# A two-layer decoder trunk: one plain feed-forward block fewer, and two unit heads side by side

## The chip, the cores and the metric

The kernel runs on one core of a Trainium2 chip. The metric is the device time of one launch in microseconds; before the change it is 1261.36 us, the median of three runs (1261.36 to 1261.72). TensorE multiplies, VectorE (DVE), ScalarE (ACT) and GpSimd (POOL) do the elementwise work, SyncE (SP) issues nearly all loads. Each engine takes its instructions in the order in which the program lists them.

## The reference

What is computed: two layers of a hybrid decoder on 512 tokens with 16 learned meta tokens ahead, model width 1024, float32.

```python
def hybrid_layer(h, ...):
    proj = rmsnorm(h, attn_norm_g) @ w_in          # 8 heads of forgetting attention, 4 of retention
    mix = concatenate([fox_out, silu(rg) * groupnorm(ret)], -1)
    h = h + mix @ w_out
    hn = rmsnorm(h, ffn_norm_g)
    ff = silu(hn @ w_gate) * (hn @ w_up)           # d_ff = 2816 = 22 blocks of 128
    return h + ff @ w_down
```

In the second layer only the 512 real tokens are needed after the attention's keys and values, and a final RMSNorm follows.

## The kernel before

**Layout.** Channels lie on the 128 partitions, tokens along the free dimension: `h` is 8 tiles of 128 x 528. Each float32 factor of a product is split into a rounded part `hi` and a rest `lo`, both of a type that TensorE takes at full rate, and a product is three matmuls: hi x hi, hi x lo, lo x hi. So each weight tile of 128 x 1024 that is loaded (`raw`) is cast by ScalarE (`whi`) and subtracted by VectorE or GpSimd (`wlo`) before TensorE can use it. A job is one such weight tile. Layer 0 takes all 528 columns as two matmuls of 264, layer 1 the 512 real ones as one matmul of 512.

**The feed-forward (`ffn`, lines 842 to 1264).** The 22 blocks of 128 hidden channels are computed in one of two ways.

- A *plain* block (`f < PLAIN`, three of them) is two jobs of `dense_steps`, gate and up, over the 8 input tiles: 96 matmuls of 264 columns in layer 0, 48 of 512 in layer 1. `g_done` scales the gate's sums and applies silu, `u_done` multiplies and splits the result into the activations `ah`, `al`.
- A *unit* (class `Unit`, line 937) does gate and up together by a Strassen-like scheme with seven half products instead of eight, 84 matmuls of half the columns (264 in layer 0, 256 in layer 1). Its four weight forms `w1` to `w4` are jobs of their own: `w1` is the gate weights, `w2` and `w3` are sums and differences of gate and up weights that VectorE makes in `make2` and `make3` (`S`, `fraw`), `w4` comes from `make4`. Its parts on TensorE are `head` (24 matmuls with `w1`, plain tokens `xh`, `xl`), `middle` (36, with `w2` and half of `w3`) and `tail` (24, with the rest of `w3` and `w4`). `middle` and `tail` need the token forms `th`, `tl`, which `x_forms` makes for four pairs of input tiles on ScalarE and VectorE while the plain blocks run. A unit holds one bank of `psa` (four banks in all) and one two-bank accumulator of `psd` (two in all); `done` (line 1002) reads it with the addition of line 1006.

**Down products.** Blocks are gathered in rounds (`ROUNDS`). When a round is complete, each of the 8 tiles of `h` gets the round's part of the down projection: four jobs of two tiles each. They are put into the next round: a unit's middle, the first down product, the unit's tail, the second down product (lines 1079 to 1106). `tails` and the loop at line 1102 serve the units that have no such job and the jobs that are left over. In layer 1 the last round is done in two column parts (272 and 240) together with the final norm.

**What sets the order.** TensorE's instructions stand in the order in which the steps are written. The other engines' are placed by a list scheduler: of what is ready by its own clock it takes what comes first in the program; `high_priority` moves a piece ahead. Buffers come from rings: `raw` has three, `whi`/`wlo` and the units' second ring `fwhi`/`fwlo` two each, jobs alternating between the two rings. `dense_steps` (line 205) casts the next job's weights at steps 1 and 4 of a job (`convert(j + 1)`), `need` (line 912) those of a unit's job and up to two after it. Steps put in from line 1259 on place the token forms and the RMS statistics among the first steps.

Of the kernel before, what the change touches and what calls it, by code (L numbers as in the profile page):

```python
# [11 lines left out]
F32R = mybir.dt.float32r  # L12
# [27 lines left out]
def hybrid_kernel(ctx, tc, x_t, w_in, w_fl, w_out, w_gate, w_up, w_down, vecs, b_fg, rope, decay, mask, ident, out_t):  # L40
# [127 lines left out]

    def wring(tag):
        pool = phase["ffn"] if tag[0] == "f" else wp  # L170
        return pool.tile([128, NK, 128], F32R, name=tag, tag=tag, bufs=2)

    def convert(j, upto=NK, pinned=False):

        if j >= len(jobs):
            return
        job = jobs[j]
        fetch(j)
        if "make" in job:
# [12 lines left out]
        while job["split"] < min(n, upto):  # L192
            c0 = job["split"]
            c1 = min(n, c0 + (2 if j < 2 and c0 < 4 else 4))
            size, hi, lo = job["w"][c0 // job["w"][0][0]]
            o = c0 % size
            hi, lo = hi[:, o:o + c1 - c0], lo[:, o:o + c1 - c0]
            with tc.high_priority() if j == 5 else ExitStack():
                pin(nc.scalar.copy(hi, job["raw"][:, c0:c1]), pinned)  # L199
            step = 1 if job["pool"] else c1 - c0  # L200
            for c in range(0, c1 - c0, step):
                pin(sub(lo[:, c:c + step], job["raw"][:, c0 + c:c0 + c + step], hi[:, c:c + step].bitcast(F32)), pinned)  # L202
            job["split"] = c1

    def dense_steps(src, parts, pool=False, banks=False, ahead=(1, 4), own=None, wait=None):

# [5 lines left out]
        def chunk(k0, k, n, xs, cols, ps, done):  # L212
            def go():
# [621 lines left out]
    def out_proj(l, rnd, mix, real):  # L835

        cols = REAL if real else FULL
        xs = lambda k: mix[k]["mix"]
        return sum([dense_steps(w_out[l, rnd, m2], [(4 * s, xs, 4, cols, add_h(2 * m2 + s, real)) for s in range(2)],
                                rnd == 0 or m2 < 2, rnd == 1 and m2 == 1) for m2 in range(NK // 2)], [])  # L840

    def ffn(l, st, real, last):
        QC = REAL if real else FULL
# [93 lines left out]
        class Unit:  # L937
# [23 lines left out]
            def make2(self, hi, lo):  # L961
                a, b = self.t["a"], self.t["b"]
                s = self.t["s"] = fft("S", F32, (128, NK, 128), 2)
                nc.vector.tensor_add(s[:, HB:NK], b[:, 0:HB], b[:, HB:NK])
                nc.vector.tensor_sub(s[:, 0:HB], s[:, HB:NK], a[:, 0:HB])
                splits(hi, lo, s)


            def make3(self, hi, lo):
# [104 lines left out]
            return [chunk(k) for k in range(n)]  # L1074

        steps = []
        tails = []
        fills = []
        for r, (f0, f1) in enumerate(ROUNDS):
            for f in range(f0, f1):  # L1080
                if f < PLAIN:
                    steps += dense_steps(w_gate[l, f], [(0, xs, NK, QC, g_done(f) if f else held.append)], banks=f == 1)
                    steps += dense_steps(w_up[l, f], [(0, xs, NK, QC, u_done(f))])
                    continue
                u = Unit(f)
                steps += u.head()
                for v in tails:
                    v.last()
                    steps += v.tail()
                tails = []  # L1090
                u.rest()
                steps += u.middle()
                if fills:
                    p, g0, g1 = fills.pop(0)
                    j = down_job(p, g0, g1)
                    steps += down(j, 0, 2 * p, g0, g1, not real)
                    u.last()
                    steps += u.tail()
                    steps += down(j, 1, 2 * p + 1, g0, g1, False)
                else:  # L1100
                    tails = [u]
            for p, g0, g1 in fills:
                j = down_job(p, g0, g1)
                for s in range(2):
                    steps += down(j, s, 2 * p + s, g0, g1, False)
            fills = [(p, f0, f1) for p in range(NK // 2)]
        n = f1 - f0
        js = [down_job(p, f0, f1) for p, _, _ in fills]
# [349 lines left out]
```

## Time and profile before

| | |
|---|---|
| median of three runs | 1261.36 us |
| profiled execution | 1261.38 us |
| its span, first to last instruction | 1259.6 us |
| mean granted clock of TensorE | 0.998 |
| idle time of TensorE | 10.9 us, of it 2.1 in the first 50 us and 8.5 in the last 60 |
| bytes moved | 116.19 MB, 92 GB/s |

The span is 1.8 us shorter than the time of the execution. The profile has one row for each group of instructions with its engine, line and tiles; PE is TensorE, PEld its weight loads, which run beside the matmuls, DVE VectorE. An instruction is shown by its start and its length, and since instructions overlap a little on their engine, the spacing of starts says how fast a queue moves. The chain of waits follows the work that ended last back to its beginning. A table of waits says who waited for whom.

### The profile page before, as it was taken

What the parts mean: (1) busy time and instruction counts of PE and PEld (TensorE: products, weight loads), DVE (VectorE), ACT (ScalarE), POOL (GpSimd) and SP (SyncE); (2) the same over time, 40 slices, a digit from 0 to 9 for tenths busy, and PEclk for the clock granted to TensorE, in tenths of its full rate; (3) what the DMA queues carried; (4) which work ended last, traced back from release to release, by engine and by line L of the source; (5) the groups of instructions that cost most, each with busy time, mean ns of one, the idle gap of its engine ahead of it and who ended that gap; (6) DMA issues with size and microseconds to landing.
All of it is one profiled execution on the core that took longest, in us unless ns stands there. A gap on an engine that the chain in (4) does not pass through costs nothing.

```text
span 1259.6 us, 23534 instructions
## 1 busy us (share of the span) xinstructions
PE 1248.7 (99%) x9225; PEld 1191.9 (95%) x9225; DVE 989.2 (79%) x1786; ACT 706.6 (56%) x1307; POOL 281.6 (22%) x552
## 2 busy tenths in 40 slices
PE   9999999999999999999999999999999999999997
PEld 8999999999999999999999988998789999999996
DVE  7887756789888888887786876567899888888867
ACT  7767655776454444444466665557764444444445
POOL 4545655420000000000125556554100000000000
PEclk9999999999999999999999999999999999999999
DMA  6222222123233323332322222221333333333322
GB/s 219 68 76 71 74 68 90 55 81 117 93 102 103 96 100 101 101 101 85 103 75 84 76 77 70 82 77 51 130 95 111 101 101 101 100 101 101 101 84 67
DMA packets 43342, 116.19 MB, mean 92 GB/s; under 512 B 5088, under 2 KB 12000, under 8 KB 43232
## 3 DMA queue, kind: packets, MB, share of 16 engines
q1 hardware_dynamic: 42800, 114.41, 28.4%
q8 instruction: 72, 1.18, 0.4%
q14 instruction: 38, 0.31, 0.1%
q10 hardware_dynamic: 432, 0.29, 0.1%
HBM read 112.58 MB, written 2.10 MB: 91 GB/s over the span
## 4 chain that ended last, share of the span: by engine, by line
PE 95%; DVE 3%; ACT 2%; DMA 0%; issue 0%; ACTq 0%; DVEq 0%
PE psd L225 31%; PE psa L930 18%; PE psd L1065 14%; PE psd L930 13%; PE psa L225 5%; PE psa L1065 4%; PE psa L441 2%; PE psa L608 2%; PE psa L538 1%; PE psa L742 1%; PE psa L778 1%; PE psa L402 1%; PE psa L304 0%; DMA raw<-w_in 0%; PE psa L617 0%
## 5 line engine op out<-in xcount | busy, mean ns | idle before, releaser
L202 POOL TENSOR_TENSOR wlo<-raw,whi 128x128 fp32r<-128x128 f32 x504 | 262.4, 555 | 243.0 <-ACT whi L199 220.9
L225 PE MATMUL psd<-xh,whi 128*128 128x264 f32 (+1 forms) x792 | 195.2, 314 | 0.1
L225 PE MATMUL psd<-xh,wlo 128*128 128x264 f32 (+1 forms) x792 | 186.6, 303 | 0.0
L225 PE MATMUL psd<-xl,whi 128*128 128x264 f32 (+1 forms) x792 | 186.2, 302 | 0.2 <-DVE xl L341 0.2
L225 PEld LDWEIGHTS psd<-xh,wlo 128*128 128x128 f32 x792 | 126.8, 188 | 6.3 <-DVE wlo L202 0.4
L225 PEld LDWEIGHTS psd<-xh,whi 128*128 128x128 f32 x792 | 128.1, 189 | 4.9 <-ACT whi L199 0.6
L225 PEld LDWEIGHTS psd<-xl,whi 128*128 128x128 f32 x792 | 127.3, 188 | 4.8 <-DVE xl L341 0.9
L199 ACT CAST whi<-raw 128x512 fp32r<-128x512 f32 (+1 forms) x168 | 98.2, 613 | 42.9 <-PE psd L225 29.2
L918 ACT CAST whi<-raw 128x1024 fp32r<-128x1024 f32 (+2 forms) x62 | 54.9, 885 | 51.3 <-PE psd L930 39.8
L918 ACT CAST fwhi<-raw 128x1024 fp32r<-128x1024 f32 (+2 forms) x62 | 55.6, 897 | 47.5 <-PE psd L930 40.0
L122 POOL MEMSET kc<- 64x528 f32 x4 | 2.1, 533 | 345.6 <-PE psa L930 345.4
L919 DVE TENSOR_TENSOR wlo<-raw,whi 128x1024 fp32r<-128x1024 f32 (+2 forms) x62 | 62.9, 1015 | 12.3 <-ACT whi L918 12.2
L919 DVE TENSOR_TENSOR fwlo<-raw,fwhi 128x1024 fp32r<-128x1024 f32 (+2 forms) x62 | 64.0, 1032 | 10.1 <-ACT fwhi L918 10.0
L930 PE MATMUL psa<-th,whi 128*128 128x264 f32 (+1 forms) x232 | 65.4, 282 | 0.0
L930 PE MATMUL psa<-th,wlo 128*128 128x264 f32 (+1 forms) x232 | 65.4, 282 | 0.0
L930 PE MATMUL psa<-tl,whi 128*128 128x264 f32 (+1 forms) x232 | 65.3, 282 | 0.0
L930 PE MATMUL psa<-th,fwhi 128*128 128x264 f32 (+1 forms) x224 | 63.4, 283 | 0.0
L930 PE MATMUL psa<-tl,fwhi 128*128 128x264 f32 (+1 forms) x224 | 63.3, 283 | 0.0
L930 PE MATMUL psa<-th,fwlo 128*128 128x264 f32 (+1 forms) x224 | 63.2, 282 | 0.0
L555 ACT ACTIVATE pr<-pr,nmax 128x144 f32<-128x144 f32 (+1 forms) x64 | 36.8, 576 | 45.5 <-DVE nmax L542 26.0
L918 ACT CAST fwhi<-S 128x1024 fp32r<-128x1024 f32 x20 | 21.0, 1049 | 68.6 <-PE psa L930 66.5
L996 ACT COPY e<-psa 128x264 f32<-128x264 f32 (+1 forms) x114 | 42.8, 375 | 28.3 <-PE psa L930 24.1
(366 smaller groups left out, 4041.1 us busy)
## 6 DMA issues: line engine op xcount, KB each, us to landing
raw<-w_in SPq DMA_DIRECT2D x54, 512.0 KB, 3.5
raw<-w_gate SPq DMA_DIRECT2D x44, 512.0 KB, 3.9
fraw<-w_up SPq DMA_DIRECT2D x38, 512.0 KB, 3.5
raw<-w_down SPq DMA_DIRECT2D x64, 256.0 KB, 2.9
raw<-w_out SPq DMA_DIRECT2D x16, 512.0 KB, 3.5
raw<-w_down SPq DMA_DIRECT2D x32, 192.0 KB, 2.5
raw<-w_up SPq DMA_DIRECT2D x6, 512.0 KB, 3.5
h<-x_t SPq DMA_DIRECT2D x8, 264.0 KB, 4.9
```

The costliest lines, as they stand in the source:

```text
L199: pin(nc.scalar.copy(hi, job["raw"][:, c0:c1]), pinned)
L202: pin(sub(lo[:, c:c + step], job["raw"][:, c0 + c:c0 + c + step], hi[:, c:c + step].bitcast(F32)), pinned)
L225: nc.tensor.matmul(ps[1][b][:, 0:c1 - c0], w[:, wk, :], x[:, c0:c1], start=(k == 0 and i == 0), stop=(k == n - 1 and i == 2))
L402: nc.tensor.matmul(ps[:, 0:c1 - c0], wf[k // HB][:, k % HB, :], st["x"][k][part][:, c0:c1], start=(i == 0), stop=(i == 2 * NK - 1))
L441: nc.tensor.transpose(ps[:, 128 * j:128 * j + 128], src[:, o:o + 128], idt)
L555: nc.scalar.activation(pr, pr, AF.Exp, bias=nmax[0:nq], scale=-1.0, accum_out=rsum)
L608: nc.tensor.matmul(po[:, c0:SEQ], v[:, j, :], pp[:, j, META + c0:T], start=(j == 0 and i == 0), stop=(j == 4))
L918: nc.scalar.copy(hi, src)
L919: nc.vector.tensor_sub(lo, src, hi.bitcast(F32))
L930: nc.tensor.matmul(bank()[:, 0:b.shape[-1]], a[:, o + k, :], b, start=(fresh and k == 0 and i == 0), stop=(k == n - 1 and i == 2), skip_gr ...
L996: nc.scalar.copy(self.t["e"][:, i], self.t["x"][:, 0:w])
L1065: nc.tensor.matmul(v[:, 0:c1 - c0], a[:, s * n + k, :], b[:, c0:c1], start=(k == 0 and i == 0), stop=(k == n - 1 and i == 2))
```

## The change

In both layers the feed-forward has two plain blocks instead of three, so the units begin with block 2. The rounds are 2 blocks and five times 4 instead of 3, four times 4 and 3: each round's four down jobs now fall on four units, and `tails` and the loop for left-over jobs are gone. At the first unit the heads of blocks 2 and 3 are both issued before the first `middle`, so two units are open at once; for these two units the first down product goes to two `psa` banks in layer 1 as well. `make2` of block 2 is put at high priority. The rings `whi` and `wlo` get three buffers. Dense jobs of the feed-forward's start cast two jobs ahead (`far`), GpSimd instead of VectorE subtracts for one more job of the second output projection (`m2 < 3`), and the token forms stand 7 steps apart instead of 9.

```diff
-ROUNDS = ((0, 3), (3, 7), (7, 11), (11, 15), (15, 19), (19, 22))
-PLAIN = 3
+ROUNDS = ((0, 2), (2, 6), (6, 10), (10, 14), (14, 18), (18, 22))
+PLAIN = 2
...
-        return pool.tile([128, NK, 128], F32R, name=tag, tag=tag, bufs=2)
+        return pool.tile([128, NK, 128], F32R, name=tag, tag=tag, bufs=2 if tag[0] == "f" else 3)
...
-                [(NK, *[wp.tile([128, NK, 128], F32R, name=i, tag=i) for i in ("whi", "wlo")])]
+                [(NK, *[wring(i) for i in ("whi", "wlo")])]
...
                 for half, at_step in enumerate(ahead):
                     if k0 + k == at_step:
                         convert(j + 1, 4 * half + 4)
+                        if far:
+                            convert(j + 2, 4 * half + 4)
...
-                                rnd == 0 or m2 < 2, rnd == 1 and m2 == 1) for m2 in range(NK // 2)], [])
+                                rnd == 0 or m2 < 3, rnd == 1 and m2 == 1, far=rnd == 1 and m2 > 1) for m2 in range(NK // 2)], [])
...
             def make2(self, hi, lo):
...
+                with tc.high_priority() if self.f == PLAIN else ExitStack():
+                    nc.vector.tensor_add(s[:, HB:NK], b[:, 0:HB], b[:, HB:NK])
+                    nc.vector.tensor_sub(s[:, 0:HB], s[:, HB:NK], a[:, 0:HB])
+                    splits(hi, lo, s)
...
-                    steps += dense_steps(w_gate[l, f], [(0, xs, NK, QC, g_done(f) if f else held.append)], banks=f == 1)
-                    steps += dense_steps(w_up[l, f], [(0, xs, NK, QC, u_done(f))])
+                    steps += dense_steps(w_gate[l, f], [(0, xs, NK, QC, g_done(f) if f else held.append)], banks=f == 1, far=True)
+                    steps += dense_steps(w_up[l, f], [(0, xs, NK, QC, u_done(f))], far=f == 0)
                     continue
-                u = Unit(f)
-                steps += u.head()
-                for v in tails:
-                    v.last()
-                    steps += v.tail()
-                tails = []
+                for i in (f, f + 1) if f == PLAIN else (f,):
+                    if i not in units:
+                        units[i] = Unit(i)
+                        steps += units[i].head()
+                u = units[f]
                 u.rest()
                 steps += u.middle()
...
+                p, g0, g1 = fills.pop(0)
                 j = down_job(p, g0, g1)
+                steps += down(j, 0, 2 * p, g0, g1, not real or f < PLAIN + 2)
+                u.last()
+                steps += u.tail()
+                steps += down(j, 1, 2 * p + 1, g0, g1, False)
...
-            steps.insert(NK + 4 + 9 * i, x_forms(i))
+            steps.insert(NK + 4 + 7 * i, x_forms(i))
```

**VectorE ahead of block 3's head, layer 0.** In before, `wlo_4558` is the low part of block 3's gate weights (`w1`), `wlo_4488` that of the third plain block's up weights, `fwlo_4605` block 3's `w2`. The queue around it is:

```order
L202 TENSOR_TENSOR wlo_4488<-raw_4485,whi_4487 128x512
L874 TENSOR_TENSOR tq_4465<-tq_4465,sg_4396 128x528
L895 SCALAR_TENSOR_TENSOR S_4503<-h7_80,vec_84,S_4503 128x264
L202 TENSOR_TENSOR wlo_4488<-raw_4485,whi_4487 128x512
L151 TENSOR_TENSOR al1_4469<-tq_4465,ah1_4468 128x528
L964 TENSOR_TENSOR S_4606<-fraw_4555 128x512
L151 TENSOR_TENSOR tl1_4288<-S_4503,th1_4287 128x1056
L865 SCALAR_TENSOR_TENSOR sg_4537<-psd_4472,R_4273 128x528
L919 TENSOR_TENSOR wlo_4558<-raw_4553,whi_4557 128x1024
```

In the changed kernel `wlo_4495` is block 2's `w2`, made from `S_4496`, and `fwlo_4491` the low part of block 3's gate weights:

```order
L967 TENSOR_TENSOR S_4496<-fraw_4360 128x512
L897 SCALAR_TENSOR_TENSOR S_4459<-h7_80,vec_84,S_4459 128x264
L968 TENSOR_TENSOR S_4496<-S_4496,raw_4358 128x512
L875 SCALAR_TENSOR_TENSOR tq_4479<-psd_4422,R_4287 128x528
L151 TENSOR_TENSOR tl1_4302<-S_4459,th1_4301 128x1056
L921 TENSOR_TENSOR wlo_4495<-S_4496,whi_4494 128x1024
L876 TENSOR_TENSOR tq_4479<-tq_4479,sg_4410 128x528
L921 TENSOR_TENSOR fwlo_4491<-raw_4486,fwhi_4490 128x1024
L151 TENSOR_TENSOR al1_4483<-tq_4479,ah1_4482 128x528
```

The low part for block 3's head now stands behind all four token forms, as before, and behind the whole of block 2's `make2` and `w2`; the dense halves between have gone, and `al1` stands behind it.

**TensorE at the first unit's second down product, layer 0.** In before the first unit (block 3) ends its tail in `psd_4631`, and the second down product goes to `psd_4768`, the other accumulator:

```order
L930 MATMUL psd_4631<-xh7_4148,whi_4676 128x264
L930 MATMUL psd_4631<-xl7_4149,whi_4676 128x264
L930 MATMUL psd_4631<-xh7_4148,wlo_4677 128x264
L1065 MATMUL psd_4768<-ah0_4326,fwhi_4647 128x264 x2
L1065 MATMUL psd_4768<-al0_4327,fwhi_4647 128x264 x2
```

In the changed kernel block 2 ends its tail in `psd_4516`, block 3's head has filled the other accumulator (`psd_4549`), and `psd_4677` lies in the banks of `psd_4516`:

```order
L932 MATMUL psd_4516<-xh7_4162,fwhi_4594 128x264
L932 MATMUL psd_4516<-xl7_4163,fwhi_4594 128x264
L932 MATMUL psd_4516<-xh7_4162,fwlo_4595 128x264
L1068 MATMUL psd_4677<-ah0_4340,whi_4565 128x264 x2
L1068 MATMUL psd_4677<-al0_4341,whi_4565 128x264 x2
```

The rows read alike, but the first matmul of `psd_4677` can start only when the addition that reads `psd_4516` has run. That addition stands in VectorE's queue behind these (`fwlo_4649` is block 3's `w3`, `S_4780` belongs to block 4):

```order
L1073 TENSOR_TENSOR h0_73<-psa_4621,h0_73 128x264
L967 TENSOR_TENSOR S_4780<-fraw_4744 128x512
L968 TENSOR_TENSOR S_4780<-S_4780,raw_4742 128x512
L974 TENSOR_TENSOR fraw_4744<-raw_4742,fraw_4744 128x512
L921 TENSOR_TENSOR fwlo_4649<-fraw_4488,fwhi_4648 128x1024
L1009 TENSOR_TENSOR sg_4665<-psd_4516,e_4514 128x528
```

So the conversions for blocks 3 and 4 have moved ahead of block 2's release of its accumulator.

More of the change, by code (lines that the diff above doesn't have):

```diff
@@ L203, in convert, with dense_steps @@
             job["split"] = c1
-    def dense_steps(src, parts, pool=False, banks=False, ahead=(1, 4), own=None, wait=None):
+    def dense_steps(src, parts, pool=False, banks=False, ahead=(1, 4), own=None, wait=None, far=False):
         j = len(jobs)
@@ L963, in make2 @@
                 s = self.t["s"] = fft("S", F32, (128, NK, 128), 2)
-                nc.vector.tensor_add(s[:, HB:NK], b[:, 0:HB], b[:, HB:NK])
-                nc.vector.tensor_sub(s[:, 0:HB], s[:, HB:NK], a[:, 0:HB])
-                splits(hi, lo, s)
+                with tc.high_priority() if self.f == PLAIN else ExitStack():
+                    nc.vector.tensor_add(s[:, HB:NK], b[:, 0:HB], b[:, HB:NK])
+                    nc.vector.tensor_sub(s[:, 0:HB], s[:, HB:NK], a[:, 0:HB])
+                    splits(hi, lo, s)
             def make3(self, hi, lo):
@@ L1076, in ffn @@
         steps = []
-        tails = []
         fills = []
+        units = {}
         for r, (f0, f1) in enumerate(ROUNDS):
```

13 lines of the change are left out of this document (removed).

## The prediction

> **What bounds the kernel now.** I read the page's engine table and chain first, then the table of waits for TensorE, then busy times by stretch.
>
> ```profile
> PE 1248.7 (99%) x9225; PEld 1191.9 (95%) x9225; DVE 989.2 (79%) x1786; ACT 706.6 (56%) x1307; POOL 281.6 (22%) x552
> PE 95%; DVE 3%; ACT 2%; DMA 0%; issue 0%; ACTq 0%; DVEq 0%
> ...
> PE psa L1300 <- DVE wide L62: 1.6, 1, 1.6
> PE psa L608 <- DVE ptl L151: 0.5, 1, 0.5
> ...
> 0.00:50.00 50.00, 47.91 (x365) 45.97 (x366) 40.69 (x88) 38.20 (x83) 25.23 (x55) 1.00 0.48 166
> 300.00:400.00 100.00, 100.00 (x826) 100.00 (x825) 88.45 (x135) 48.46 (x70) 0.00 (x0) 1.00 0.33 105
> 900.00:1000.00 100.00, 99.98 (x621) 89.21 (x620) 93.41 (x144) 55.03 (x82) 0.00 (x0) 1.00 0.35 111
> 1100.00:1200.00 100.00, 100.00 (x698) 93.23 (x698) 82.48 (x119) 46.72 (x66) 0.00 (x0) 1.00 0.32 101
> 1200.00:1260.00 60.00, 51.50 (x358) 47.72 (x357) 40.42 (x74) 28.34 (x55) 0.00 (x0) 0.95 0.22 71
> ```
>
> TensorE idles 10.9 us of 1259.6, nearly all in the first 50 us (2.1) and the last 60 (8.5). Inside the feed-forward it never waits. So a gain can come only from fewer or shorter matmuls, and a loss from any wait that the change makes. In a row of a stretch, its length is followed by the busy times of PE, PEld, DVE, ACT and POOL, then by granted clock, DMA share and GB/s. VectorE is at 82% in the steady units of layer 1, but 93% in the stretch that holds the plain blocks and the token forms. That stage has little VectorE time to give, and the change shortens it.
>
> **What is saved.** The chain shows the spacing of matmuls of each width.
>
> ```profile
> 299.95 17.36 PE psd L225 x144
> 317.31 1.45 PE psa L930 x12
> 921.32 16.59 PE psd L225 x72
> 937.92 1.43 PE psa L930 x12
> 1218.37 2.76 PE psd L1065 x12
> 1232.28 12.04 PE psa L930 x99
> ```
>
> Layer 0 (264 columns): 17.36/144 = 0.1206 us for a plain matmul, 1.45/12 = 0.1208 in a unit. A plain block has 96 (11.57 us), a unit 84 (10.15): 1.43 saved. Layer 1: a plain block has 48 matmuls of 512 columns at 16.59/72 = 0.2304 (11.06), a unit 84 of 256 at 0.119 or a little less (9.95): 1.11 saved. Against that, block 2's and 3's first down products of layer 1 are cut in two halves: 12 x 0.119 for 6 x 2.76/12, twice, +0.1. The last round has 4 blocks instead of 3, and its matmuls are in two column parts: 24 pairs at about 2 x 12.04/99 = 0.243 instead of 0.230 at most, +0.3, +0.2 taken. Net saving 1.43 + 1.11 - 0.3 = 2.2 us. It is certain, being work that TensorE no longer has.
>
> **The wait at the second head.** One block fewer means 11.57 us less TensorE cover for VectorE in layer 0, and the second head (block 3) must start one head after the first. How long VectorE takes per instruction is read from starts that follow each other, since it ran without a gap there.
>
> ```profile
> 303.37 0.43 DVE L862 SCALAR_TENSOR_TENSOR sg<-psa,R 128x264 f32<-128x264 f32 x1
> 303.71 0.49 DVE L895 SCALAR_TENSOR_TENSOR S<-h,vec,S 128x264 f32<-128x264 f32 x1
> ...
> 310.18 0.68 DVE L964 TENSOR_TENSOR S<-fraw 128x512 f32<-128x512 f32 x1
> 310.78 1.25 DVE L151 TENSOR_TENSOR tl<-S,th 128x1056 fp32r<-128x1056 f32 x1
> 311.95 0.70 DVE L865 SCALAR_TENSOR_TENSOR sg<-psd,R 128x528 f32<-128x528 f32 x1
> 312.56 1.22 DVE L919 TENSOR_TENSOR wlo<-raw,whi 128x1024 fp32r<-128x1024 f32 x1
> 313.70 0.68 DVE L965 TENSOR_TENSOR S<-S,raw 128x512 f32<-128x512 f32 x1
> 317.39 0.28 PE L930 MATMUL psa<-xh,wlo 128*128 128x264 f32 x1
> ...
> 934.32 1.22 DVE L919 TENSOR_TENSOR wlo<-raw,whi 128x1024 fp32r<-128x1024 f32 x1
> 935.46 0.69 DVE L965 TENSOR_TENSOR S<-S,raw 128x512 f32<-128x512 f32 x1
> 937.99 0.28 PE L930 MATMUL psa<-xh,wlo 128*128 128x256 f32 x1
> ```
>
> That gives 0.34 us for 264 columns, 0.60 for 512 or 528, 1.14 for 1024, 1.17 for 1056. In before the low part of block 3's gate weights is done at 313.70 and the head's third matmul, the first to read it, starts at 317.39: 3.7 us to spare; 2.5 in layer 1 (935.46, 937.99).
>
> After: that matmul is due at 317.39 - 11.57 + 24 x 0.1208 = 308.72. By VectorE's queue as the order shows it, ahead of this low part (`fwlo_4491`) no longer stand the six half weights of three dense jobs (6 x 0.60), block 2's gate scaling (0.6) and the low part of block 1's activation (0.6), together 4.8; newly there stand block 2's own two low parts of 1024 (`wlo_4363`, `wlo_4495`, 2 x 1.14) and the subtraction for its second weights (0.6), together 2.9. So it is done at 313.70 - 4.8 + 2.9 = 311.8, and TensorE, in order, stands 3.1 us. The cover is gone, not the work. In layer 1: due 937.99 - 11.06 + 24 x 0.119 = 929.8, done 935.46 - 4.2 + 2.9 = 934.2 (the activation's low part stays ahead): 4.4 us. The ends: 0.5 less each if ScalarE and VectorE pack better than in before, 0.6 more each for a cast that ScalarE now has to give first.
>
> **The wait for a bank.** With two units open both 2-bank accumulators are taken, so block 2's second down product (`psd_4677`) has to wait until `sg<-psd,e` has read block 2's sums; behind it on TensorE stands everything else. In before it took the other accumulator.
>
> ```profile
> 330.39 0.70 DVE L1006 TENSOR_TENSOR sg<-psd,e 128x528 f32<-128x528 f32 x1
> 1249.33 0.28 PE L930 MATMUL psa<-ah,fwlo 128*128 128x240 f32 x1
> 1249.78 0.40 DVE L1123 TENSOR_TENSOR h<-psa,h 128x240 f32<-128x240 f32 x1
> ...
> raw<-w_gate SPq DMA_DIRECT2D x44, 512.0 KB, 3.9
> ```
>
> At the least it costs the handover (1249.78 against the matmul's end at 1249.61, 0.2), the addition (0.7) and the handover back (0.1): 1.0 us. By the queues: TensorE goes on at 311.85 with 22 + 36 + 12 + 24 matmuls, 11.4 us, and is there at 323.2. VectorE has from 311.8 thirteen instructions of 0.60, three of 1.14 and three of 0.34, 12.2 us, ahead of the addition: 324.0, done 324.7. So 1.5 us. In layer 1: 94 x 0.119 from 934.3 is 945.5; VectorE has twelve, three and three, 11.6 us from 934.2, and waits about 1.2 in the middle, because block 4's gate weights load (3.9 us) into the buffer that block 2's last low part gives back 5.9 us after 934.2. Done 934.2 + 12.8 + 0.7 = 947.7: 2.2 us; 1.0 without that wait. The upper ends are again 0.6 more each.
>
> **Edits that cost nothing.** GpSimd takes out-projection job 2:
>
> ```profile
> 263.59 2.21 POOL L202 TENSOR_TENSOR wlo<-raw,whi 128x128 fp32r<-128x128 f32 x4 [2.25 <-ACT whi L199]
> 269.98 0.40 PE L225 MATMUL psd<-mxh,whi 128*128 128x264 f32 x2
> ```
>
> Eight at 0.55 us from 265.8 end at 270.2; the first are done long before 269.98. If its cast came late, 0.5 us. The third weight buffer and the two jobs of lookahead only move casts earlier, beside matmuls; SP's loads still go out when one of three raw buffers is given back. No wait that they could remove is in the table. In the steady units VectorE's queue has at least the 18% of slack above, and each conversion stands as far ahead of its matmuls as before: nothing. The last round's longer products could take 0.3 us off the tail after them, or nothing.
>
> **The sum.** The profiled execution took 1261.4 us (span 1259.6), the median is the same. 1261.4 - 2.2 + 3.1 + 4.4 + 1.5 + 2.2 = 1270.4 us. With the waits at their lower ends (2.6, 3.9, 1.0, 1.0) it is 1267.7, at their upper (3.7, 5.0, 2.1, 2.8) 1272.8.
>
> **Rivals.** *Waits that also cost clock* (0.12). The last stretch shows 0.95 for 60 us with 8.5 idle, 3 us of clock lost; the first, with 2.1 us idle, 1.00. At 0.35 per idle us the two head waits cost 1.1 and 1.5 more: 1273.0. It decides if the granted clock drops right behind a head wait. The Trainium skill (TensorE: Matmul & The Clock Gate, Part 1: The HAM clock gate) says that the clock halves after an idle window of about 3.4 us and comes back after a busy one of that length; by it only layer 1's 4.4 us could trip it, for an estimated 1.7 us. The two rows fit that rule, but show no gap of this size between matmuls.
>
> *Only the bank wait* (0.08). If VectorE comes to the second heads in time, because the job given to GpSimd and the earlier casts let it start the stage some 3 to 4 us ahead, what is left is 2 x 1.0: 1261.2, no change. Against it: VectorE ran without a gap over the whole stage, and what stands ahead in its queue needs TensorE's sums of the out projection, which come no earlier.
>
> *Faster* (0.08). The same lead, and the bank handed over behind the matmuls still in TensorE's pipeline: 1261.4 - 2.2 = 1259.2. It decides if neither `fwlo` at the second head nor `psd` at the down product shows a wait. For it speaks that the saving is sure; against it that the addition cannot begin before the last matmul that it reads has ended.
>
> **How the numbers follow.** The forecast has 0.72. About 0.2% (2.5 us) is what a measurement of this kernel can tell from no change. The range runs from 1264, which lets half of both kinds of waits be hidden, to 1274, the clock case and the upper ends. Slower by over 0.2%: 0.72 + 0.12 = 0.84; within: 0.08; faster: 0.08, its case lying right at that bound.
>
> **What would show it.** In the changed kernel (line numbers are its own), TensorE's table of waits should have two lines for line 932, on VectorE's `fwlo` (3.1 and 4.4 us), and two for line 1068, on the addition of line 1009 (1.5 and 2.2), and nothing else new; 84 x 2 matmuls of line 932 more. VectorE should show no gap in the 30 us ahead of the second heads. The forecast is wrong if line 932's first wait is under 1 us, or if waits of some size stand in the later units, where I count none.

## The result, and the profile after

The changed kernel takes 1281.25 us (median of five runs, 1279.52 to 1282.7) against 1261.57 (1261.36 to 1261.93): a ratio of 1.0153, interval 1.0139 to 1.0168. It is slower, by 19.7 us where the forecast had 9, and it lies outside the range. The profiled execution took 1279.52 us with a span of 1277.7, so it is the fastest of the five.

Two lines of the page of the changed kernel matter first, the engine table and the chain's shares.

```profile
PE 1251.5 (98%) x9285; PEld 1198.2 (94%) x9285; DVE 993.8 (78%) x1799; ACT 710.0 (56%) x1313; POOL 292.9 (23%) x568
PE 88%; DVE 8%; ACT 3%; issue 1%; DMA 1%; ACTq 0%; SPq 0%; DVEq 0%
```

TensorE's share of the chain fell from 95% to 88%, and VectorE's rose from 3% to 8%. TensorE is busy for 1251.5 of 1277.7 us, so it idles 26.2 us where it idled 10.9.

TensorE's table of waits says where (us in total, times, longest):

```profile
PE psa L932 <- DVE fwlo L921: 7.7, 2, 4.5
PE psd L1068 <- DVE sg L1009: 3.0, 2, 1.5
PE psa L932 <- ACT ah L150: 2.2, 1, 2.2
PE psd L1068 <- ACT ah L150: 1.4, 1, 1.4
...
PE psa L932 <- DVE al L151: 0.3, 1, 0.3
PE psd L1068 <- DVE al L151: 0.2, 1, 0.2
```

The first two lines are the four waits of the forecast: the second head in each layer (3.2 and 4.5 us) and the first unit's second down product (1.5 and 1.5). The other four, 4.1 us together, were not forecast at all. They stand at the end of the last round of each layer: the activations `ah` and `al` of the last unit come late.

The stretches of the changed kernel (length, then busy time of PE, PEld, DVE, ACT and POOL, then granted clock, DMA share and GB/s) around the heads and around layer 1's end:

```profile
300.00:320.00 20.00, 16.78 (x139) 16.57 (x138) 19.96 (x31) 10.39 (x16) 0.00 (x0) 1.00 0.18 63
...
940.00:944.00 4.00, 2.78 (x13) 2.78 (x14) 4.00 (x6) 1.29 (x2) 0.00 (x0) 0.50 0.11 32
...
1245.00:1250.00 5.00, 5.00 (x30) 5.00 (x29) 1.65 (x4) 1.69 (x4) 0.00 (x0) 0.66 0.02 3
```

VectorE has no gap while TensorE waits for the head (19.96 of 20 us), as the forecast said. The clock is the second thing that its sum left out: half speed behind layer 1's head wait, and again behind the wait at the end of layer 1, at 1245 to 1250, while the matmuls run. The chain shows it in the matmuls behind layer 1's head wait (start, us, what, count):

```profile
941.22 2.50 PE psa L932 x10
943.73 2.29 PE psd L932 x12
946.02 1.41 PE psa L932 x12
```

Twenty-two take 4.79 us, where the last row's pace would make it 2.6.

The chain of the changed kernel through layer 1's end (start, us, what) shows what makes `ah` late:

```profile
1238.55 0.69 DVE sg L1009
1239.23 1.13 DVE fwlo L921
...
1243.18 0.63 ACT ah L150
...
1243.83 0.70 DVE al L151
```

From the first addition behind the last unit's tail to `ah` are 5.3 us, the low part of the next down weights (1.13) among them, and 0.7 more to `al`. In the kernel before, the chain at the same place runs on matmuls alone:

```profile
1223.96 8.31 PE psd L1065 x36
```

Thirty-six matmuls stand behind the last unit there: 12 of its own second down product and 24 of the left-over down job, 8.3 us, and the same chain of VectorE and ScalarE hides under them. The change gives the last round four blocks, so that no job is left over. Then only 12 matmuls (2.8 us) and the first three blocks of the last products stand there.

### The profile page after: what moved, and what is told of

Same layout as the page of the kernel before. It is cut to its first block, busy times and chain, and to the rows that moved or that the text cites. A ratio compares the mean times of both kernels' runs of the same rounds, so it can differ in the third digit from the quotient of the medians.

```text
span 1277.7 us, 23634 instructions
## 1 busy us (share of the span) xinstructions
PE 1251.5 (98%) x9285; PEld 1198.2 (94%) x9285; DVE 993.8 (78%) x1799; ACT 710.0 (56%) x1313; POOL 292.9 (23%) x568
## 4 chain that ended last, share of the span: by engine, by line
PE 88%; DVE 8%; ACT 3%; issue 1%; DMA 1%; ACTq 0%; SPq 0%; DVEq 0%
PE psd L225 26%; PE psa L932 19%; PE psd L1068 13%; PE psd L932 13%; PE psa L1068 4%; PE psa L225 4%; PE psa L443 2%; PE psa L610 2%; PE psa L540 1%; PE psa L744 1%; PE psa L780 1%; DVE fwlo L921 1%; DVE tl L151 1%; DVE wlo L921 1%; DMA h<-x_t 0%
## 5 line engine op out<-in xcount | busy, mean ns | idle before, releaser
L202 POOL TENSOR_TENSOR wlo<-raw,whi 128x128 fp32r<-128x128 f32 x520 | 273.9, 561 | 590.2 <-ACT whi L199 584.8
L225 PE MATMUL psd<-xh,whi 128*128 128x264 f32 (+1 forms) x744 | 182.4, 313 | 0.0
L225 PE MATMUL psd<-xh,wlo 128*128 128x264 f32 (+1 forms) x744 | 173.8, 302 | 0.0
L225 PE MATMUL psd<-xl,whi 128*128 128x264 f32 (+1 forms) x744 | 173.6, 301 | 0.0
L920 ACT CAST whi<-raw 128x1024 fp32r<-128x1024 f32 (+1 forms) x64 | 57.0, 890 | 102.0 <-PE psa L932 65.2
L921 DVE TENSOR_TENSOR wlo<-raw,whi 128x1024 fp32r<-128x1024 f32 (+1 forms) x64 | 65.2, 1018 | 30.3 <-ACT whi L920 30.2
L920 ACT CAST fwhi<-raw 128x1024 fp32r<-128x1024 f32 (+1 forms) x64 | 57.0, 890 | 50.8 <-PE psd L932 42.2
L921 DVE TENSOR_TENSOR fwlo<-raw,fwhi 128x1024 fp32r<-128x1024 f32 (+1 forms) x64 | 65.2, 1018 | 5.8 <-ACT fwhi L920 5.8
L1075 DVE TENSOR_TENSOR h<-psd,h 128x512 f32<-128x512 f32 (+1 forms) x66 | 45.7, 693 | 12.6 <-PE psd L1068 12.5
L1068 PE MATMUL psd<-ah,whi 128*128 128x264 f32 (+1 forms) x180 | 50.5, 329 | 4.5 <-DVE sg L1009 3.0
```

What stands on the lines that cost most here:

```text
L225: nc.tensor.matmul(ps[1][b][:, 0:c1 - c0], w[:, wk, :], x[:, c0:c1], start=(k == 0 and i == 0), stop=(k == n - 1 and i == 2))
L920: nc.scalar.copy(hi, src)
L921: nc.vector.tensor_sub(lo, src, hi.bitcast(F32))
L1068: nc.tensor.matmul(v[:, 0:c1 - c0], a[:, s * n + k, :], b[:, c0:c1], start=(k == 0 and i == 0), stop=(k == n - 1 and i == 2))
L1075: nc.vector.tensor_add(sv(h[m], real), pv(ps[0], real), sv(h[m], real))
```

## The experiments

Times are medians in us; the kernel before was run beside each and took 1261.3 to 1261.6.

| kernel | time | runs | ratio, interval |
|---|---|---|---|
| changed | 1281.25 | 1279.5 to 1282.7 | 1.0153, 1.0139 to 1.0168 |
| no priority | 1278.63 | 1275.7 to 1279.5 | 1.0133, 1.0118 to 1.0148 |
| one head | 1271.44 | 1270.4 to 1273.9 | 1.0082, 1.0067 to 1.0098 |
| plain jobs on GpSimd | 1281.57 | 1279.2 to 1283.2 | 1.0155, 1.0138 to 1.0172 |
| end covered | 1277.13 | 1276.5 to 1278.2 | 1.0126, 1.0111 to 1.0141 |
| one wait filled | 1281.30 | 1279.3 to 1283.4 | 1.0155, 1.0139 to 1.0171 |
| all waits filled | 1276.29 | 1276.0 to 1276.6 | 1.0115, 1.0098 to 1.0131 |
| one head, end covered | 1267.15 | 1267.0 to 1267.5 | 1.0043, 1.0028 to 1.0058 |
| the same, no priority | 1271.16 | 1270.8 to 1271.4 | 1.0074, 1.0059 to 1.0089 |
| two buffers again | 1280.35 | 1279.6 to 1281.1 | 1.0151, 1.0134 to 1.0168 |
| before, other rounds | 1270.69 | 1270.3 to 1271.0 | 1.0072, 1.0055 to 1.0088 |
| before, three buffers | 1265.81 | 1264.3 to 1266.3 | 1.0030, 1.0018 to 1.0041 |

My theory had three parts: (1) at the head of the stage VectorE is the limit, and opening two units there makes TensorE stand for it; (2) at the end the left-over job was the cover of the last unit's activations; (3) the rest is clock, lost behind waits. The rivals were that VectorE is late over the whole stage, so that a wait cured in one place comes back in another, and that the clock has nothing to do with the waits.

**One head only.** The second unit's head goes back behind the first unit.

```diff
-                for i in (f, f + 1) if f == PLAIN else (f,):
+                for i in (f,):
```

> The changed kernel with block 3's head behind block 2, as the other heads stand. Theory: the two waits for the accumulator (1.5 us each) go, since one unit is open at a time; block 2's middle, due 2.9 us sooner, waits for its own second weights, about 2 us in layer 0 and 3 in layer 1, in place of 3.2 and 4.5: 1275 to 1277 us. Rival (two heads ahead are what hides the token forms): the wait at the middle is as long as both heads' cover, 5 us and more, and the time rises over 1281.

Measured: 1271.44, 9.8 us less, and better than I expected. TensorE's waits at line 932 in this kernel:

```profile
PE psa L932 <- DVE fwlo L921: 1.5, 2, 0.8
...
PE psa L932 <- DVE wlo L921: 1.1, 2, 0.8
```

With 1.3 of three smaller rows, 3.9 us stand where 10.7 stood (7.7 and 3.0), and the bank wait has no row left. No single wait at the head is over 0.8 us now, and its granted clock is 1.00 from 300 to 340 and from 930 to 970 us, which fits the rest of the gain. So opening two units makes 6.8 of the 10.7 us; the 3.9 that stay belong to the missing plain block and to the rest of the change together.

**No priority for the first unit's second weights.**

```diff
-                with tc.high_priority() if self.f == PLAIN else ExitStack():
+                with ExitStack():
```

> The changed kernel, with block 2's second weights at normal priority. By VectorE's order the low part for block 3's head then stands ahead of them. Theory (VectorE in arrears; TensorE waits at whichever head or middle is first short of weights): the waits at block 3's head (3.2 and 4.5 us) go, and waits of about 2.3 and 3.4 us come at block 2's middle: 2 us less, and about 2 more if the drop of the clock behind the 4.5 us wait goes with it: 1277 to 1279 us against 1281. Rival (only the order is wrong, there are no arrears): both go, 1271 us.

Measured: 1278.63, 2.6 less, as the theory had it. The wait moves rather than goes. The table of this kernel:

```profile
PE psa L932 <- ACT whi L920: 2.8, 2, 1.8
...
PE psa L932 <- DVE wlo L921: 1.5, 2, 0.8
```

The head's `fwlo` is 0.2 now, and block 2's middle waits instead for its second weights, 4.3 us in all: the same VectorE work in another order.

**The plain jobs' low parts on GpSimd.** VectorE is rid of the half weights of these jobs.

```diff
-                    steps += dense_steps(w_up[l, f], [(0, xs, NK, QC, u_done(f))], far=f == 0)
+                    steps += dense_steps(w_up[l, f], [(0, xs, NK, QC, u_done(f))], True, far=f == 0)
```

and the same in the line for `w_gate`.

> The changed kernel with the low parts of the four plain jobs' weights on GpSimd: VectorE has 8 x 0.6 = 4.8 us less to do ahead of the second heads. Theory (arrears of VectorE): the waits at the heads (3.2 and 4.5 us) and the clock lost behind the second (about 2 us) go, the waits for the accumulator shrink to 1.0 each, the end of the rounds stays: 1281 - 9.7 - 1 = 1270 us. Rival (the waits come from the order or from ScalarE's casts): under 3 us less. Rival (GpSimd at 4.4 us a job is too slow): waits of TensorE's line 225 on GpSimd, no gain.

Measured: 1281.57, no gain. The head waits did go, but others came, 7.4 us in three rows, above all this one of its table, in the plain blocks:

```profile
PE psd L225 <- DVE sg L867: 4.8, 2, 3.6
```

The timeline of its VectorE (start, us, line, what), while GpSimd subtracts beside it, shows why:

```profile
276.46 0.96 DVE L343 SCALAR_TENSOR_TENSOR xl<-h,vec,xh 128x528 fp32r<-128x528 f32 x1
277.35 0.96 DVE L363 TENSOR_TENSOR ss<-ss,sq 128x528 f32<-128x528 f32 x1
278.23 0.69 DVE L834 TENSOR_TENSOR h<-psd,h 128x528 f32<-128x528 f32 x1
278.85 0.77 DVE L363 TENSOR_TENSOR ss<-ss,sq 128x528 f32<-128x528 f32 x1
```

Behind the first two, which have both tensors in SBUF, the next operation starts after 0.89 and 0.88 us, where the prediction counted 0.60 and the kernel before has 0.68 and 0.61; behind the third, which reads a sum from PSUM, it starts after 0.62, as before. The fourth has both in SBUF too, but takes 0.77 us where the first two take 0.96; why it is spared stays open. GpSimd pays too. Its own row of the timeline:

```profile
271.15 18.26 POOL L202 TENSOR_TENSOR wlo<-raw,whi 128x128 fp32r<-128x128 f32 x24 [5.09 <-ACT whi L199]
```

That is 0.76 us each, against 0.55 in the kernel before. So much of the work that left VectorE's queue came back as time of what stayed in it. The Trainium skill (SBUF — State Buffer, Who interferes with whom) says that a VectorE instruction with two SBUF inputs contends with a GpSimd instruction that reads SBUF, and that one with at most one SBUF input does not, outside the modes that use two ports. The first three rows agree, the fourth does not show it.

**The end covered.** The last unit's first down product goes behind its tail, in both layers, so that in layer 1 24 matmuls stand behind that unit, where the changed kernel has 12 and the kernel before 36.

```diff
-                steps += down(j, 0, 2 * p, g0, g1, not real or f < PLAIN + 2)
+                first = down(j, 0, 2 * p, g0, g1, not real or f < PLAIN + 2)
                 u.last()
-                steps += u.tail()
+                steps += u.tail() + first if f == NF - 1 else first + u.tail()
```

> The changed kernel, with the last unit's first down product moved behind its tail in both layers. Theory (the last round's first product needs the last unit's activations, which nothing covers since the left-over down job is gone): 2.9 us more of cover each; the waits there (1.6 and 2.5 us) go, and 1.6 us of clock lost behind the second: 1281 - 5.7 = 1275.5 us. Rival (the activations are late because VectorE is behind, and would be as late again behind the tail): no change.

Measured: 1277.13, 4.1 less, where the theory had 5.7. The rows on `ah` and `al` are gone, and those of the head (7.7) and the bank (3.0) are as they were. What is new is small:

```profile
PE psa L932 <- ACT e L999: 0.9, 2, 0.5
```

The waits fell by 4.1 - 0.9 = 3.2. Its profile lost clock at another place, 0.94 over 310 to 340 us, where the changed kernel's shows 1.00, which fits the smaller gain.

**The kernel before with other rounds.** This makes the end of the rounds alone: three plain blocks and nothing else of the change, but the round of three comes second, and so its left-over job too.

```diff
-ROUNDS = ((0, 3), (3, 7), (7, 11), (11, 15), (15, 19), (19, 22))
+ROUNDS = ((0, 3), (3, 6), (6, 10), (10, 14), (14, 18), (18, 22))
```

> The kernel before with its three plain blocks, no new buffers or lookahead, and only its table of rounds changed, so that the round of three blocks comes second and the last has four: the left-over down job then stands in the third round's end and no longer behind the last unit. Theory (that left-over job is what covered the activations of the last unit): TensorE waits at line 930 and line 1065 for ah and al at the end of each layer, 1.6 us in layer 0 and 2.5 in layer 1, 4.1 in all, with up to 1.6 of lost clock behind the second: 1265.4 to 1267. Rival (the end of the rounds is not what costs; the waits there come from VectorE being late since the head of the stage): no such wait, 1261.3 within 0.5.

Measured: 1270.69, 9.1 more, about twice what the theory gave and far from the rival. The table of waits of this kernel has just two rows that the kernel before has not:

```profile
PE psa L930 <- ACT ah L150: 3.1, 1, 3.1
...
PE psd L1065 <- ACT ah L150: 2.1, 1, 2.1
```

These are 5.2 us. Behind each the clock went down: 0.91 over the 20 us from 620 and 0.69 over the 5 us from 1235, 1.8 and 1.6 us. That is 8.6 of the 9.1, and 0.5 more is what two waits cost beside their rows (shown below). So the mechanism is shown, and its size depends on what VectorE has in hand at that moment: here one more low part (1.13 us) stood ahead of the activations.

**One head and the end covered.** Both mends together.

> The changed kernel with one head ahead of the token forms' chain instead of two, and with the last unit's first down product behind its tail, both mends that ran alone before. Theory (the two losses are apart, one at the head of a stage and one at its end): the gains add, 1271.4 less 4.1 is 1267.3. Rival (VectorE is the limit over the whole stage, and what one wait gives back the next takes): less than half of the second gain, 1269.5 or more.

Measured: 1267.15, where the sum gave 1267.3. The two losses are apart. The largest waits that the change still makes, in this kernel's table:

```profile
PE psa L932 <- DVE fwlo L921: 1.5, 2, 0.8
PE psa L932 <- DVE wlo L921: 1.2, 2, 0.8
```

None is over 0.8 us, and the runs are 0.5 us apart. Yet it is still slower than the kernel before, by 5.6 us. The rows of its table add up to 8.2 us, those of before to 2.7: 5.5 more. Against that stand 2.4 us of saved matmuls, by a count given with the point on the saving below, so this explains 3.1 of the 5.6. The rest is about what the waits cost beside their rows: there are 14 of them here and 5 in the kernel before, and each costs some 0.26 us more than its row says, as the waits of known length below show. For nine that is 2.3 us.

**The same without the priority.**

> The changed kernel with one head, the last unit's first down product behind its tail, and without the priority of the first unit's second weights. Theory (VectorE's order in the stage is what is left to gain; without two heads the priority pushes block 2's low part ahead of work that TensorE needs sooner): the sum of the waits at lines 225, 932 and 1068 falls from about 6 us to about 4, and the time to 1265.5. Rival (with one head the priority is needed, and taking it away moves the wait to block 2's middle): 1268 or more.

Measured: 1271.16, the rival. With one head the priority is needed. The table of this kernel:

```profile
PE psa L932 <- ACT fwhi L920: 4.0, 2, 3.5
```

One of these waits, in layer 1, is 3.5 us long, and the clock is 0.83 over 930 to 950. All rows of the table are 10.6 us, 2.4 more than in the last kernel; the rest of the four us between the two fits the clock that was lost behind that wait.

**Two buffers again.** The third buffer, the two jobs of lookahead and GpSimd's out-projection job 2 are undone in the changed kernel.

```diff
-        return pool.tile([128, NK, 128], F32R, name=tag, tag=tag, bufs=2 if tag[0] == "f" else 3)
+        return pool.tile([128, NK, 128], F32R, name=tag, tag=tag, bufs=2)
...
-                                rnd == 0 or m2 < 3, rnd == 1 and m2 == 1, far=rnd == 1 and m2 > 1) for m2 in range(NK // 2)], [])
+                                rnd == 0 or m2 < 2, rnd == 1 and m2 == 1) for m2 in range(NK // 2)], [])
...
```

> The changed kernel with three of its parts undone: two buffers for the high and low parts, one job of lookahead, and out-projection job 2 back on VectorE; the blocks, the heads and the rounds stay as changed. The forecast counted these parts at nothing. Theory (they are nothing: in the changed kernel no wait on TensorE hangs on a free buffer): 1281.3 within the 1.7 us that the runs of the changed kernel lie apart, with the head waits, the bank waits and the end waits as they were. Rival (they hide something: with two buffers block 2's gate and second weights cannot be cast while the last plain job's are in use, and VectorE has 1.2 us more in the out projection): head waits longer by 1 us or more each, 1284 or more. Against both: in the kernel before, the same parts alone cost 4.2 us, because GpSimd then took layer 1's first low parts ahead of small memsets that ScalarE waited for between the layers; if the changed kernel pays for that too, it falls here.

Measured: 1280.35, within the spread. The waits shift, but not in sum:

```profile
PE psa L932 <- DVE fwlo L921: 6.5, 2, 5.2
PE psa L932 <- ACT ah L150: 3.1, 1, 3.1
```

With the bank's 2.3 and layer 0's end (2.1) they are 14.0 us, and 14.3 in the changed kernel (7.7, 2.2, 3.0 and 1.4). More buffers take 1.6 us off the end and put 1.9 on the head.

**The kernel before with three buffers.** The same parts put into the kernel before: these lines the other way round, and `far=f < PLAIN - 1` at the line for `w_up`.

> The kernel before with the third buffer for the high and low parts, two jobs of lookahead in the plain jobs and in part of the out projection, and out-projection job 2 on GpSimd, and nothing else of the change. Theory (these only move casts that lie beside matmuls): 1261.3 within 0.6, with no new row in TensorE's table of waits. Rival (earlier casts bring the feed-forward's start forward, or take ScalarE and GpSimd from the attention's own steps): 1 us or more either way.

Measured: 1265.81, 4.2 more, where the theory had no change. Its one new wait of size is in the norm between the layers:

```profile
PE psa L306 <- ACT sqh L150: 2.1, 1, 2.1
```

and ScalarE's timeline there says for whom ScalarE waits:

```profile
646.16 0.22 ACT L150 CAST mxh<-wfr 128x32 fp32r<-128x32 f32 x1 [3.72 <-POOL mxh L388]
646.28 0.63 ACT L150 CAST sqh<-ss 128x528 fp32r<-128x528 f32 x1
```

With a free buffer GpSimd takes layer 1's first low parts ahead of a memset for which a small cast on ScalarE waits, and in this kernel that cast stands ahead of `sqh`. The clock is 0.91 over the 20 us behind it. In the changed kernel `sqh` stands ahead of that cast, and there is no such wait. So "nothing" held for the change, but by that order, which I had not looked at.

**One wait filled.** In layer 1, just ahead of the second head, 32 matmuls that nothing reads.

```diff
+                    if real and k == 0 and o == 0 and j == units[PLAIN + 1].w1:
+                        idle = psum_a()
+                        for _ in range(32):
+                            nc.tensor.matmul(idle[:, 0:xh.shape[-1]], ones, xh, start=True, stop=True)
```

> The changed kernel with 32 extra matmuls of 256 columns ahead of block 3's head in layer 1, whose sums nothing reads: about 3.8 us of TensorE work that lies inside the 4.5 us for which TensorE stands there anyway. It changes no result and takes no wait of VectorE away. Theory (the clock halves behind that wait, and twenty-two matmuls at about 0.2 us in place of 0.119 cost 2 us): the granted clock stays at 1.00 between 938 and 946 us, and the time falls by about 2 us against the changed kernel, to 1279.3. Rival (the slow matmuls behind the wait are late for another reason, say VectorE's operands): no change, 1281.3, and the extra matmuls could even cost a few tenths if they hold up the head.

Measured: 1281.30, the rival's number, but not its reason. The clock in this kernel's profile (a run of 1282.96):

```profile
936.00:948.00 12.00, 11.27 (x91) 10.90 (x90) 11.89 (x18) 5.33 (x8) 0.00 (x0) 1.00 0.08 22
950.00:970.00 20.00, 18.02 (x131) 17.32 (x130) 17.18 (x28) 8.31 (x13) 0.00 (x0) 0.91 0.39 124
310.00:320.00 10.00, 7.29 (x47) 7.29 (x48) 8.67 (x12) 3.55 (x7) 0.00 (x0) 0.83 0.31 88
...
620.00:635.00 15.00, 13.32 (x95) 12.90 (x94) 11.13 (x18) 8.16 (x12) 0.00 (x0) 0.89 0.36 107
```

At 936 to 948 it is 1.00 now, as meant. But it was lost behind the bank wait at 957, and in layer 0 behind the head and the end, where this kernel is the same as the changed one and the changed one's profile shows 1.00. One and the same wait costs clock in one run and not in another.

**All waits filled.** Matmuls that nothing reads in each of the six new places: 24 and 32 ahead of the heads, 8 and 10 ahead of the bank waits, 12 and 18 at the ends.

```diff
+        def fill(count, x):
+            idle = psum_a()
+            for _ in range(count):
+                nc.tensor.matmul(idle[:, 0:x.shape[-1]], ones, x, start=True, stop=True)
...
```

> The changed kernel with extra matmuls, whose sums nothing reads, in every place where TensorE stands newly: 24 and 32 ahead of block 3's head (2.9 and 3.8 us), 8 and 10 ahead of the second down product (about 1 us each), 12 and 18 ahead of the first matmul that reads the last unit's activations (1.4 and 2.1 us). The waits stay as long for the rest of the program; only TensorE is busy in them. The single dummy of before (layer 1's head alone) left the time where it was, and its profile lost clock in four other places. Theory (the clock is lost behind whichever of these waits comes at a bad moment, 1.5 to 2 us each time, two to four times in a run, and that is also why the runs lie 3 us apart): granted clock 1.00 from 100 to 1260 us, time near 1276 (the profiled 1279.5 less the 3.6 us that its clock lost), runs within 1 us of each other. Rival (the clock is lost whether or not TensorE stands, or the extra matmuls delay the work behind them by as much): 1279 to 1283 and the spread as before.

Measured: 1276.29, all runs within 0.5 us. The clock of this kernel from 100 to 1260 us, and its largest wait of the change:

```profile
100.00:1260.00 1160.00, 1157.14 (x8582) 1106.30 (x8581) 902.25 (x1590) 631.20 (x1131) 235.35 (x455) 1.00 0.28 88
```
```profile
PE psa L937 <- DVE fwlo L921: 1.0, 2, 0.7
```

The matmuls put in are useless and the time falls by 5.0 us. The rest of the program waits as long as before; TensorE just does not stand. So about 5.0 us of the median are clock, and so is the spread: the runs of the changed kernel lie 3.2 us apart, these 0.5.

**Waits of known length.** In the kernel before, 24 waits in the steady units of both layers: a matmul, 1 to 8 memsets of GpSimd that wait for it, and a matmul that waits for them. Nothing reads their sums. It ran once.

```diff
+                b = psum_a()
+                nc.tensor.matmul(b[:, 0:256], ones, slow[:, 0:256], start=True, stop=True)
+                for _ in range(count):
+                    nc.gpsimd.memset(slow.bitcast(F32), 1.0)
+                b = psum_a()
+                nc.tensor.matmul(b[:, 0:256], ones, slow[:, 0:256], start=True, stop=True)
...
```

> The kernel before with 24 waits of known length put into the steady units, where it has none: one matmul, 1 to 8 memsets of GpSimd of 128x512 (about 0.5 us each) that wait for it, and one matmul that waits for them; each length in both layers, and 1, 3, 5 and 7 twice in each. Nothing reads these sums. It measures by itself how long a wait must be to cost clock, and how much. Theory (a wait of 2 us or more can halve the clock for about 3 us behind it, at a cost of 1.5 us, and one of under 1 us never does): no half clock behind 1 memset, half clock behind some of those with 3 and more, behind nearly all with 7 and 8. Rival (only a wait of over 3.4 us can do it): half clock behind 7 and 8 memsets alone.

Measured: 1364.22 us, with 63.6 us in the 24 waits. Two of them, the first with the matmul that follows it, and the stretches of 12 us around five:

```profile
486.57 0.38 PE L1086 MATMUL psa<-slow,ones 128*128 128x256 f32 x1 [1.87 <-POOL slow L1084]
486.79 0.29 PE L933 MATMUL psa<-th,fwhi 128*128 128x264 f32 x1
1154.14 0.39 PE L1086 MATMUL psa<-slow,ones 128*128 128x256 f32 x1 [1.86 <-POOL slow L1084]
```
```profile
549.00:561.00 12.00, 10.72 (x88) 10.73 (x89) 8.38 (x13) 5.42 (x8) 1.05 (x2) 1.00 0.24 75
484.00:496.00 12.00, 10.13 (x71) 9.93 (x71) 6.60 (x10) 3.87 (x5) 1.58 (x3) 0.86 0.13 37
1152.00:1164.00 12.00, 10.13 (x73) 9.32 (x72) 7.94 (x12) 4.96 (x7) 1.57 (x3) 1.00 0.21 52
525.00:537.00 12.00, 7.80 (x43) 7.59 (x43) 3.59 (x7) 2.10 (x2) 3.68 (x7) 0.72 0.00 0
1190.00:1202.00 12.00, 7.80 (x41) 6.95 (x40) 4.39 (x7) 2.10 (x2) 3.67 (x7) 0.86 0.01 2
```

A wait costs a little more than its row: the matmul ahead of it runs its full 0.28 us, where the next would have started after 0.12, and the matmul behind the one that waited starts after 0.22 (486.57 to 486.79). That is 0.26 us beside any loss of clock. The wait of two memsets at 549 (1.28 us) costs no clock. The two of 1.87 and 1.86 are alike, and one loses 0.14 of 12 us (1.7 us), the other nothing. The two of seven memsets (4.20 us each, at 525 and 1190) lose 3.4 and 1.7. Over all 24, read microsecond by microsecond, the loss is always 0, 1.7 or 3.4 us, that is no, one or two stretches of 3.4 us at half speed:

| wait, us | waits | one stretch | two |
|---|---|---|---|
| 0.64 to 1.28 | 6 | 0 | 0 |
| 1.86 to 2.16 | 4 | 2 | 0 |
| 2.45 to 3.61 | 8 | 8 | 0 |
| 4.20 | 4 | 1 | 3 |
| 4.78 | 2 | 0 | 2 |

Whole stretches, and chance at 1.9 and 4.2 us, look like a clock that is decided afresh every 3.4 us, so that it matters how a wait lies across these steps. The clock's own records in the kept traces show the steps: in each trace the half-speed stretches behind waits last 3.413 or 6.827 us, and they start at whole multiples of 3.413 us from each other. Laid over the matmuls of the eleven kernels that have such stretches, from 40 us on, these steps give a rule. After a step at full speed in which TensorE stood for 1.79 us or more, about half of it, the next was at half speed in all 33 cases; with 1.67 to 1.78 us in 4 of 6; with up to 1.55 us in none of 3864. The wait of 1.87 us lies whole in one step, that of 1.86 us is split into 1.23 and 0.64. So was the changed kernel's own head wait of 3.2 us in layer 0, into 1.44 and 1.78, and behind it the profile shows 1.00. The Trainium skill (TensorE: Matmul & The Clock Gate, Part 1: The HAM clock gate) says that the window is 3413 ns long and free-running. The 3.4 us agree. That it takes an idle window of that length does not: a wait of 1.87 us was enough here.

## Why the prediction was wrong, point by point

- **The saving (2.2 us).** No run measures it alone, but it can be counted: with each matmul of the two traces at the usual spacing of its size in the kernel before, the matmuls take 1236.1 us before and 1233.7 after, 2.4 less. With it the account of the 19.7 us closes: the rows of TensorE's table add up to 17.9 us against 2.7, 15.2 more; seven more waits cost about 1.8 beside their rows; the clock cost 5.0 in the median. 15.2 + 1.8 + 5.0 - 2.4 = 19.6.
- **The second heads (3.1 and 4.4).** Measured 3.2 and 4.5, by the mechanism named: VectorE without a gap, the cover gone. The one-head run takes the wait away.
- **The bank (1.5 and 2.2).** Measured 1.5 and 1.5. With one head there is no such wait. In layer 1 the size came near by luck, since two errors offset each other: TensorE came 2.2 us later than I had it, by the clock lost behind the head, and VectorE took 14.9 us from the head's low part to the end of the addition (941.1 to 956.0), where I had 13.5.
- **Edits that cost nothing.** This is the step that failed, where it says that in the steady units each conversion stands as far ahead of its matmuls as before. I looked at how far weights are cast ahead of their matmuls, and not at the activations, which have no lookahead. The diff takes out the loop that emits the left-over down job; I counted that job's matmuls as kept, and not that they were the cover of the last unit. By rows of before it could have been seen: 36 matmuls, 8.3 us, behind the last unit, against a chain of about 6 us through VectorE and ScalarE. It is 4.1 us of waits, and the changed rounds alone make such waits in the kernel before (5.2 us).
- **Waits that also cost clock.** This rival was right, and 0.12 was too little for it. Its price was 2.6 us, for the heads alone; measured are 5.0 in the median, about three stretches of 1.7, behind any of the six waits of 1.4 us and more. I weighed it by a row that averaged the whole end of the kernel.
- **The buffers, the lookahead and GpSimd's job.** Nothing in the sum, as forecast, though they move about 1.6 us from one wait to another.
- **Only the bank wait; faster.** Neither came near. VectorE started the stage no earlier.

So 9 us of the 19.7 were forecast by mechanism and nearly by size (10.7 of waits less 2.4 saved are 8.3); the end of the rounds brought 4.1, the clock 5.0, and some 2 what the waits cost beside their rows. No version here is faster than the kernel before: the best, with both mends, is at 1.0043 (1.0028 to 1.0058).

## What to carry to other kernels

When a change takes work off the engine that sets the time, list what that work hid, at every place where it stood, and not only where it is taken out: here the left-over job at the end of the rounds was the cover of a chain of 6 us. Matmuls that stand directly behind a long chain of other engines are cover even if they look like a remainder. And count every wait on TensorE as 0.26 us more than its row, and one of 1.7 us and more, or shorter ones that add up to that within 3.4 us, as 1.7 us of clock more, with a chance that grows with its length; a wait over 4 us can cost that twice.

## What the runs showed of the hardware

- The clock's loss comes in whole stretches of 3.4 us at half speed (1.7 us each, if matmuls run in them): in 0 of 6 waits up to 1.28 us, 2 of 4 around 1.9 us and all 14 from 2.45 us on of the waits of known length, though behind the changed kernel's 3.2 us in layer 0 there was none. It is decided in steps of 3.413 us: half speed follows a step in which TensorE stood for about half of it (33 of 33 from 1.79 us on, none of 3864 up to 1.55). Runs of one kernel differ by that: 3.2 us where six such waits stand, 0.5 where they are filled or gone.
- Matmuls that nothing reads, put where TensorE would stand, made the kernel 5.0 us faster.
- A wait of TensorE costs about 0.26 us beside its row and any clock: 0.28 in place of 0.12 for the matmul ahead of it, 0.22 in place of 0.12 for the one that waited.
- With GpSimd subtracting beside it, most of VectorE's operations on two SBUF tensors of 528 columns took 0.88 to 0.89 us in place of 0.61 to 0.68, and GpSimd's own 0.76 in place of 0.55; operations that read PSUM stayed at 0.62.
